# Operand tiles at one place of a 512-byte line, sums rounded together with their residues, and other steps for transposing activations, in a hybrid attention and convolution block

## The chip, the cores and the metric

One core of a Trainium2 chip runs the whole kernel. The metric is the device time of one execution in microseconds; of several runs the median is given. Lower is better.

## The reference

One layer of a streaming encoder on 256 tokens of width 2048, in float32:

```
xn = rms_norm(x) * g1
q, k, v, ga, gg = split(xn @ w_in)            # w_in: 2048 x 5120
att = diff_attention(rope(norm(q)), rope(norm(k)), v)       # 4 heads
u   = silu(layer_norm(conv31(ga * sigmoid(gg))))            # 1024 channels
h = x + concat(att, u) @ w_out                # w_out: 2048 x 2048
hn = rms_norm(h) * g2
y = h + (silu(hn @ w_gate) * (hn @ w_up)) @ w_down          # hidden width 5632
```

## The kernel before

**Three products for one.** Each weight and each activation is split into a rounded part (`hi`, in the type that TensorE takes in one pass) and a residue (`lo`). A product is hi x hi + lo x hi + hi x lo, so one weight tile is used by three matmuls for each half of 128 tokens. The activation is the stationary operand, 128 x 128; the weight is the moving one, 128 x 512. ACT makes the rounded parts of weights (`round_chunk`, L307: `whi`; `round_pair`, L880 and L881: `wh`) and VectorE (DVE) the residues (`split_chunk`, L316: `wlo`; `split_pair`, L885 and L886: `wl`). In a few chunks the residue is made by ACT and an accumulating DMA on POOL's queue instead (L310, L311).

**A list of chunks.** All matmul work is a list, `chunks`, in the order of the stages: QKV and convolution columns (`w_in`), output projection (`w_out`), and the FFN. `run_chunks` walks it. At step t it first issues `split` of chunk t+2, then `load` and `round` of chunk t+3 (in the FFN blocks; elsewhere both lead by 2), then `multiply` of chunk t. Each engine works its own queue in that order of issue; an instruction that waits holds up those behind it.

**Generators and resumes.** What follows a product (norms, activations, transposes) is written as generators. `resume()` lets each go on to its next `yield`; it is called inside and behind each `multiply`. `lag(n)` yields n times. So a number of lags fixes the place of an instruction in the queues.

**The FFN.** The hidden width is 11 blocks (j = 0 to 10) of 512 columns. Block 0 is plain. Blocks 1 to 10 (`fast_block`) compute gate and up together, with sums and differences of operands as in a Strassen product, in 12 units, in the order `sggsggsuusuu` (block 1: `gugusgsusgsu`). A unit `s` is a pair (`multiply_pair`): seven products of three matmuls (L902, L903, L904), the stationary operands from `fhi` and `flo`, the moving ones from `wh` and `wl`, each of seven slices: three are weights as loaded, four are sums of weights (`wt`, made by DVE at L877 to L879 in `round_pair`). The second product already uses the sums. A unit `g` or `u` has two rows of weights (`multiply_two`, L919, L920, L925: 12 matmuls), the stationary operands from `chi` and `clo`. A pair has four resumes, a two-row unit two: in its middle and at its end.

**PSUM.** There are four banks with the tag `acc` and four with the tag `aux`. A block sums in all eight (`q0` to `q3` are acc, `q4` to `q7` aux). The fourth product of a pair sums in `q3`.

**From block to activation.** `products_done` starts when a block's last pair is done: it copies one bank on ACT (L964), adds the banks on DVE (L966 to L973) and applies silu on ACT (L972, L974). `block_done` starts with the block's last unit and is resumed at once: DVE adds the last two banks (L982), multiplies by the gate (L984), then comes `lag(TO_TRANSPOSE)`, and `transposed` turns 128 x 128 squares by TensorE in two groups of four (L796, into a bank `ps_a`). Each group is rounded by ACT (L798, `ahi`), its residue made by DVE (L800, `alo`). While the next block runs, three aux banks hold its sums, so both groups use the one that is left. Block 0's groups use acc banks.

**Down-projection.** Behind blocks 3, 7 and 10 (`FGROUPS` is 4, 4, 3) the products with `w_down` follow, chunks of two rows of 128 and 12 matmuls (`multiply`, L346, L347, L352), with the transposed activations as stationary operand. They have two resumes each. Those of the last group take the last block's second group in the sixth chunk.

**Where tiles lie.** Tiles of a pool lie one behind the other in each partition's memory, and pools follow each other in the order in which they are opened. By the addresses of the compiled program, the place of a tile's first byte in a line of 512 bytes is 192 for the pools `lhs` (`xhi`, `ahi`, `hhi` and their residues) and `wp` (`raw`, `whi`, `wlo`); behind them comes `small` with 1984 bytes, and so the place is 128 for `early` (`wb`) and for `ffn` (`chi`, `fhi`, `wh`, `wl`, `wt`). In `pre`, the odd sizes of `cw` (992 bytes) and `upad0`, `upad1` (4576 each) leave the stationary operands of `w_out`, `mchi`, `mclo`, `mahi` and `malo`, at 32. The latter two hold the attention output of the first two heads, the former two that of the convolution. All slices used by matmuls are whole steps of 512 bytes.

Of the kernel before, what the change touches and what calls it, by code (L numbers as in the profile page):

```python
# [12 lines left out]
F32 = mybir.dt.float32  # L13
# [5 lines left out]
P = 128  # L19
D = 2048  # L20
S = 256
# [5 lines left out]
CC = 1024  # L27
NCT = CC // P
W = 31
FF = 5632  # L30
KD = D // P
N = 512
EPS = 1e-6
LN_EPS = 1e-5
LAMBDA_INIT = 0.8 - 0.6 * math.exp(0.0)
# [31 lines left out]
FGROUPS = (4, 4, 3)  # L67
# [15 lines left out]

HI_AHEAD, LO_AHEAD = 3, 2

TO_TRANSPOSE = 5


def rope_constants():
# [10 lines left out]
def tile_block(  # L100
# [6 lines left out]
    act, dve, pool, pe, sp = nc.scalar, nc.vector, nc.gpsimd, nc.tensor, nc.sync  # L107

    const = ctx.enter_context(tc.tile_pool(name="const", bufs=1))
    lhs = ctx.enter_context(tc.tile_pool(name="lhs", bufs=KD // 2))  # L110
    wp = ctx.enter_context(tc.tile_pool(name="wp", bufs=4))
    small = ctx.enter_context(tc.tile_pool(name="small", bufs=4))
    early = ctx.enter_context(tc.tile_pool(name="early", bufs=2))
    prestack = ExitStack()
    pre = prestack.enter_context(tc.tile_pool(name="pre", bufs=2))
# [12 lines left out]
    def warm_up(n):  # L128
        warm = aux_ps.tile([P, N], F32, tag="aux", name="ps_warm")
        for _ in range(n):  # L130
            pe.transpose(warm[:, :P], ident, ident)
# [9 lines left out]
    def gain_columns():  # L141
        ps = aux_ps.tile([P, N], F32, tag="aux", name="ps_cols")
        pe.transpose(ps[:, :NR], rows, ident[:NR, :NR])
        act.copy(cols, ps[:, :NR])
# [1 line left out]
    def col(key, k):  # L146
        return cols[:, AT[key] + k : AT[key] + k + 1]

    cw = pre.tile([P, NCT, W], F32, tag="cw", name="cw", bufs=1)
    gcs = {}  # L150
    neg_lam = const.tile([P, 1], F32, tag="neg_lam", name="neg_lam")
    cw_rows = [pre.tile([W, N], F32, tag="va", name="cw_rows") for _ in range(CC // N)]
    rt = pre.tile([P, NM, 2, DH], F32, tag="vb", name="rt")
# [3 lines left out]
    def late_loads():  # L157
        flat = conv_w.rearrange("o w i c -> (o w i) c")
        for i in range(CC // N):
            sp.dma_start(out=cw_rows[i], in_=flat[:, i * N : (i + 1) * N])  # L160
        for t, v in ((gb, vecs[:2]), (lamv, vecs[2:])):
# [3 lines left out]
    def late_constants():  # L165
        late_loads()
        yield from lag(4)
        pw = aux_ps.tile([P, N], F32, tag="aux", name="ps_cw")
        for ct in range(NCT):
# [31 lines left out]
    def rsqrt_mean(dst, ss, n, eps):  # L201

        k = dst.shape[-1]
        t = small.tile([P, 8], F32, tag="rsq", name="rsq")
        pool.tensor_scalar(t[:, :k], ss, 1.0 / n, eps, ALU.mult, ALU.add)
        pool.tensor_tensor(dst, t[:, :k], neghalf[:, :k], ALU.pow)
# [8 lines left out]
    def lhs_two(pfx, k):  # L215
        return tuple(lhs.tile([P, 2, S], F32R, tag=f"l{x}", name=f"{pfx}{x}{k}") for x in ("hi", "lo"))
# [20 lines left out]
    def lag(n):  # L237
        for _ in range(n):
            yield
# [182 lines left out]
    def x_rest():  # L422
# [9 lines left out]
        for m in range(NM):  # L432
            ss = small.tile([P, 1], F32, tag="ss1", name="ss1")
            dve.tensor_reduce(ss, ss1[m], AX.X, ALU.add)
            rsqrt_mean(rstd1[m], ss, D, EPS)
        yield
# [4 lines left out]

    NB = N // P
    HN = N // 2
    upad = [pre.tile([P, NB, S + W - 1], F32, tag=f"upad{b}", name=f"upad{b}", bufs=1) for b in range(CC // N)]
    for b in range(CC // N):
        pool.memset(upad[b][:, :, : W - 1], 0.0)
    y = pre.tile([P, NCT, S], F32, tag="y", name="y", bufs=1)
# [126 lines left out]
    def qk_rows(key, b, m, ps):  # L574
# [6 lines left out]
        f = small.tile([P, G], F32, tag="fq", name="fq")  # L581
        rsqrt_mean(f, ss, DH, EPS)
        pool.tensor_scalar(f, f, rstd1[m], 0.0, ALU.mult, ALU.add)
# [102 lines left out]
    def attend_values(hd):  # L686
# [14 lines left out]
        r = small.tile([P, NM], F32, tag="ro", name="ro")  # L701
        rsqrt_mean(r, ss, E, EPS)
        yield from lag(2)
# [24 lines left out]
    def out_done(n, ps):  # L728
# [26 lines left out]
        if n == D // N - 1:  # L755
            yield
            for m in range(NM):
                ss = small.tile([P, 1], F32, tag="ssh", name="ssh")
                dve.tensor_reduce(ss, ss2[m], AX.X, ALU.add)
                rsqrt_mean(rstd2[m], ss, D, EPS)  # L760
            yield
# [16 lines left out]
    def up_done(j, ps):  # L778
        fp = ffn["pool"]
        yield  # L780
        aa = []
        for m in range(NM):
            a = fp.tile([P, N], F32, tag=f"sum{2 + m}", name="a")
            dve.scalar_tensor_tensor(a, ps[m], rstd2[m], sil[m], ALU.mult, ALU.mult)
            aa.append(a)
        yield
        yield from transposed(j, aa)

    def transposed(j, aa):
        for t in range(N // P // 2):  # L790
            pool_, tag = (aux_ps, "aux") if j else (acc_ps, "acc")
            pt = pool_.tile([P, 2, S], F32, tag=tag, name="ps_a")
            for i in range(2):
                for m in range(NM):
                    c = (2 * t + i) * P
                    pe.transpose(pt[:, i, m * P : (m + 1) * P], aa[m][:, c : c + P], ident)  # L796
            hi, lo = lhs_two("a", j * (N // P) + 2 * t)
            act.copy(hi, pt)  # L798
            yield from lag(2)
            dve.tensor_tensor(lo, pt, hi.bitcast(F32), ALU.subtract)  # L800
            for i in range(2):
                actT[j * (N // P) + 2 * t + i] = (hi[:, i, :], lo[:, i, :])
            yield from lag(2 if j else 1)

# [63 lines left out]
    def round_pair(c):  # L870

        fp = ffn["pool"]
        assert "hi" in forms
        b = c["b"]
        c["t"] = t = fp.tile([P, 4, N], F32, tag="wt", name="wt")
        c["hi"] = fp.tile([P, 7, N], F32R, tag="wh", name="wh", bufs=2)
        dve.tensor_tensor(t[:, 2:4], b[:, 1:3], b[:, 0:1].to_broadcast([P, 2, N]), ALU.subtract)  # L877
        dve.tensor_tensor(t[:, 1], b[:, 1], t[:, 3], ALU.add)
        dve.tensor_tensor(t[:, 0], t[:, 1], b[:, 3], ALU.subtract)  # L879
        act.copy(c["hi"][:, 4:], b[:, 1:])  # L880
        act.copy(c["hi"][:, :4], t)  # L881

    def split_pair(c):
        c["lo"] = ffn["pool"].tile([P, 7, N], F32R, tag="wl", name="wl", bufs=2)
        dve.tensor_tensor(c["lo"][:, 4:], c["b"][:, 1:], c["hi"][:, 4:].bitcast(F32), ALU.subtract)  # L885
        dve.tensor_tensor(c["lo"][:, :4], c["t"], c["hi"][:, :4].bitcast(F32), ALU.subtract)  # L886
# [44 lines left out]
    def fast_block(j, order, after_down):  # L931

        units, sums = [], {}
        left = dict(s=list(range(NS)), g=list(TWOS), u=list(TWOS))
        for kind in order:
            what = left[kind].pop(0)
            c = dict(kind=kind, sums=sums, done=None, first={}, last={})
            if kind == "s":
                c.update(k=what, col=j * N, load=load_pair, round=round_pair, split=split_pair,
                         multiply=multiply_pair, uses=[q for q, _, _ in PRODUCTS], products=PRODUCTS)  # L940
            else:
                c.update(ks=what, w=w_gate if kind == "g" else w_up, nk=2, width=N, cols=[(j * N, N)],
                         rows=slice(what[0], what[1] + 1, what[1] - what[0]), by_dma=j > 1 and what in BY_DMA,
                         load=load_chunk, round=round_chunk, split=split_chunk, multiply=multiply_two,
                         uses=(Q3, QX) if kind == "u" else (Q2, Q4))
            units.append(c)
        assert not any(left.values())
        if after_down:

            units[0]["products"] = PRODUCTS[4:] + PRODUCTS[:4]  # L950
        for q in range(8):
            users = [c for c in units if q in c["uses"]]
            users[0]["first"][q] = users[-1]["last"][q] = True
        [c for c in units if c["kind"] == "s"][-1]["done"] = products_done
        units[-1].update(done=lambda sums: block_done(j, sums), prompt=True)
        chunks.extend(units)
# [20 lines left out]
    def block_done(j, q):  # L977
        while "g" not in halfway:
            yield
        g, u = halfway.pop("g"), halfway.pop("u")  # L980
        for m, i in enumerate((Q3, QX)):
            dve.tensor_tensor(u[m], q[i], u[m], ALU.add)  # L982
        for m in range(NM):
            dve.tensor_tensor(u[m], u[m], g[m], ALU.mult)  # L984
        yield from lag(TO_TRANSPOSE)
        yield from transposed(j, u)

    def down_done(g, n, ps):
# [82 lines left out]
```

## Time and profile before

| | |
|---|---|
| median of 3 runs | 1084.51 us (1084.17 to 1084.56) |
| the profiled execution | 1082.97 us, span 1081.2 us |
| mean granted TensorE clock | 0.994 |
| QKV, convolution, attention | about 7 to 252 us |
| output projection | about 252 to 352 us |
| FFN block 0 | about 352 to 398 us |
| blocks 1 to 3, down-projection | 398 to 534, 534 to 622 us |
| blocks 4 to 7, down-projection | 622 to 793, 793 to 881 us |
| blocks 8 to 10, down-projection | 881 to 1008, 1008 to 1077 us |

The profile's busy share of TensorE counts modelled ends of pipelined matmuls; the distance from one start to the next tells the pace. A row of the timeline has the start in us, the duration in us, the engine, the line with the operation, what is written from what is read, the shape, how many instructions are merged, and in brackets the idle time before with what ended it. A row of the windows has the stretch, its length, busy time of TensorE with its count, granted clock, DMA share and GB/s. A row of the waits has the sum in us, the count and the longest.

### The profile page before, as it was taken

How to read it: one execution, taken by the hardware profiler on the slowest of the kernel's cores; microseconds unless marked ns; L12 is line 12 of the kernel's file. 1: busy time of each engine (PE TensorE's matmuls, PEld its weight loads, DVE VectorE, ACT ScalarE, POOL GpSimd, SP SyncE). 2: the span in 40 equal slices, each digit the busy share in tenths (PEclk: the TensorE clock that was granted, in tenths of full speed). 3: DMA queues.
4: the chain of work that ended last, by engine and by line, in shares of the span. 5: the costliest groups of instructions: out<-in, count | busy, mean ns of one | idle time of the engine just before them, and what ended most of it. 6: DMA issues, size and time to landing. Idle time of an engine off the chain costs nothing.

```text
span 1081.2 us, 13236 instructions
## 1 busy us (share of the span) xinstructions
PE 1058.5 (98%) x4834; PEld 871.7 (81%) x4834; DVE 844.8 (78%) x1025; ACT 587.0 (54%) x765; POOL 62.9 (6%) x101
## 2 busy tenths in 40 slices
PE   7999999999999999999999999999999999999998
PEld 7888888877888887788888888878788888887786
DVE  4799989898765689988754699889865589898553
ACT  6544567755765655555443456554643355556332
POOL 0030021200100000000000000000000000000000
PEclk9999999999999999989999999999999999999999
DMA  8856655454345565576555776767566568675661
GB/s 244 258 178 201 190 186 172 151 167 156 137 156 195 163 240 201 195 215 194 175 200 189 238 252 211 214 202 238 164 195 215 201 216 249 220 221 161 220 220 62
DMA packets 120941, 212.45 MB, mean 196 GB/s; under 512 B 7220, under 2 KB 29166, under 8 KB 120876
## 3 DMA queue, kind: packets, MB, share of 16 engines
q1 hardware_dynamic: 117744, 200.56, 56.0%
q0 software_dynamic: 3072, 11.01, 4.9%
q8 instruction: 38, 0.62, 0.2%
q14 instruction: 27, 0.22, 0.1%
q10 hardware_dynamic: 60, 0.03, 0.0%
HBM read 200.04 MB, written 2.10 MB: 187 GB/s over the span
## 4 chain that ended last, share of the span: by engine, by line
PE 79%; DVE 10%; issue 4%; ACT 3%; DMA 2%; POOL 1%; SPq 0%; DVEq 0%; ACTq 0%
PE acc L347 16%; PE acc L346 16%; PE acc L352 16%; PE q L919 5%; PE q L920 5%; PE q L902 5%; PE q L904 5%; PE q L903 5%; PE q L925 5%; DVE wlo L316 3%; ACT wh L881 2%; DVE wt L877 1%; DVE y L483 1%; DMA h<-in_x_dram 1%; PE ps_a L796 1%
## 5 line engine op out<-in xcount | busy, mean ns | idle before, releaser
L316 DVE TENSOR_TENSOR wlo<-raw,whi 128x1024 fp32r<-128x1024 f32 (+1 forms) x279 | 337.6, 1218 | 138.0 <-ACT whi L307 138.0
L307 ACT CAST whi<-raw 128x1024 fp32r<-128x1024 f32 (+1 forms) x297 | 309.3, 1049 | 234.1 <-PE acc L347 166.4
L347 PE MATMUL acc<-whi,alo 128*128 128x512 f32 x384 | 149.6, 390 | 2.3 <-DVE alo L800 2.3
L346 PE MATMUL acc<-whi,ahi 128*128 128x512 f32 x384 | 149.6, 390 | 0.0
L881 ACT CAST wh<-wt 128x2048 fp32r<-128x2048 f32 x40 | 76.6, 1914 | 127.3 <-DVE wt L879 127.3
L346 PE MATMUL acc<-whi,xhi 128*128 128x512 f32 (+1 forms) x352 | 129.8, 375 | 3.9 <-ACT xhi L221 2.8
L347 PE MATMUL acc<-whi,xlo 128*128 128x512 f32 (+1 forms) x352 | 128.2, 371 | 0.5 <-DVE xlo L222 0.4
L919 PE MATMUL q<-whi,chi 128*128 128x512 f32 x320 | 125.7, 393 | 0.0
L920 PE MATMUL q<-whi,clo 128*128 128x512 f32 x320 | 125.4, 392 | 0.0
L902 PE MATMUL q<-wh,fhi 128*128 128x512 f32 x280 | 112.4, 402 | 2.2 <-DVE alo L800 2.2
L904 PE MATMUL q<-wl,fhi 128*128 128x512 f32 x280 | 111.2, 397 | 1.4 <-DVE wl L886 1.4
L903 PE MATMUL q<-wh,flo 128*128 128x512 f32 x280 | 110.6, 395 | 0.0
L483 DVE SCALAR_TENSOR_TENSOR y<-upad,cw,y 128x256 f32<-128x256 f32 x240 | 103.4, 481 | 2.2 <-ACT y L476 1.7
L352 PE MATMUL acc<-wlo,ahi 128*128 128x512 f32 x384 | 103.6, 391 | 0.0
L886 DVE TENSOR_TENSOR wl<-wt,wh 128x2048 fp32r<-128x2048 f32 x40 | 91.6, 2290 | 9.2 <-ACT wh L881 9.2
L352 PE MATMUL acc<-wlo,xhi 128*128 128x512 f32 (+1 forms) x352 | 88.2, 375 | 1.2 <-DVE wlo L316 1.2
L925 PE MATMUL q<-wlo,chi 128*128 128x512 f32 x320 | 87.1, 394 | 0.0
L347 PEld LDWEIGHTS acc<-whi,alo 128*128 128x128 f32 x384 | 72.1, 188 | 17.6 <-DVE alo L800 2.6
L346 PEld LDWEIGHTS acc<-whi,ahi 128*128 128x128 f32 x384 | 72.1, 188 | 15.2 <-ACT ahi L798 0.2
L352 PEld LDWEIGHTS acc<-wlo,ahi 128*128 128x128 f32 x384 | 71.6, 188 | 14.5
L346 PEld LDWEIGHTS acc<-whi,xhi 128*128 128x128 f32 x352 | 66.3, 188 | 15.8 <-ACT xhi L221 3.2
L347 PEld LDWEIGHTS acc<-whi,xlo 128*128 128x128 f32 x352 | 66.3, 188 | 11.9 <-DVE xlo L222 0.9
(194 smaller groups left out, 1416.6 us busy)
## 6 DMA issues: line engine op xcount, KB each, us to landing
raw<-in_w_down_dram SPq DMA_DIRECT2D x88, 512.0 KB, 3.9
raw<-in_w_in_dram SPq DMA_DIRECT2D x48, 512.0 KB, 3.5
raw<-in_w_gate_dram SPq DMA_DIRECT2D x48, 512.0 KB, 4.4
raw<-in_w_up_dram SPq DMA_DIRECT2D x48, 512.0 KB, 3.5
wb<-in_w_up_dram SPq DMA_DIRECT2D x40, 512.0 KB, 3.8
wb<-in_w_gate_dram SPq DMA_DIRECT2D x40, 512.0 KB, 5.6
raw<-in_w_out_dram SPq DMA_DIRECT2D x32, 512.0 KB, 3.5
raw<-in_w_in_dram SPq DMA_DIRECT2D x62, 256.0 KB, 3.4
```

The source lines that it names most:

```text
L307: act.copy(c["hi"], c["raw"])
L316: dve.tensor_tensor(c["lo"], c["raw"], c["hi"].bitcast(F32), ALU.subtract)
L346: pe.matmul(ps[m], xhi[:, ms], hi[:, j, :], start=c["first"] and j == 0, stop=False)
L347: pe.matmul(ps[m], xlo[:, ms], hi[:, j, :], start=False, stop=False)
L352: pe.matmul(ps[m], xhi[:, ms], lo[:, j, :], start=False, stop=c["last"] and j == nk - 1)
L483: dve.scalar_tensor_tensor(y[:, ct, :], src, wk, y[:, ct, :], ALU.mult, ALU.add)
L902: pe.matmul(ps, fhi[:, f, p, :], c["hi"][:, w], start=bool(first), stop=False)
L903: pe.matmul(ps, flo[:, f, p, :], c["hi"][:, w], start=False, stop=False)
L904: pe.matmul(ps, fhi[:, f, p, :], c["lo"][:, w], start=False, stop=bool(last))
L919: pe.matmul(ps, x1[:, ms], hi[:, i, :], start=i == 0 and bool(c["first"].get(q)), stop=False)
L920: pe.matmul(ps, x2[:, ms], hi[:, i, :], start=False, stop=False)
L925: pe.matmul(sum_bank(c, q), forms["plain"][k][0][:, ms], lo[:, i, :], start=False, stop=i == 1 and bool(c["last"].get(q)))
```

## The change

- `small` is opened ahead of `lhs`, and `cw` and `upad` are padded to whole lines of 512 bytes. By the sizes above, all operand tiles then begin at place 128.
- ACT's rounding of the four sums of a pair (L881) is issued in `split_pair`, one step later, right ahead of the residues that use it, instead of in `round_pair`.
- The lags around the transposes change. Behind `block_done`: 4 resumes instead of 5; between a group's rounding and its residue 2 as before; from there to the second group 4 instead of 2. For the blocks ahead of a down-projection and for block 0 (`FIRSTS` is 1, 4, 8, 11, compared with j + 1): 3, 1 and 1 (block 0 has no first lag; it had 2 and 1).

```diff
+LINE = 128
-TO_TRANSPOSE = 5
+FIRSTS = [1] + [sum(FGROUPS[: g + 1]) for g in range(len(FGROUPS))]
...
+    small = ctx.enter_context(tc.tile_pool(name="small", bufs=4))
     lhs = ctx.enter_context(tc.tile_pool(name="lhs", bufs=KD // 2))
     wp = ctx.enter_context(tc.tile_pool(name="wp", bufs=4))
-    small = ctx.enter_context(tc.tile_pool(name="small", bufs=4))
...
-    cw = pre.tile([P, NCT, W], F32, tag="cw", name="cw", bufs=1)
+    cw = pre.tile([P, LINE * 2], F32, tag="cw", name="cw", bufs=1)[:, : NCT * W].rearrange("p (c w) -> p c w", c=NCT)
...
-    upad = [pre.tile([P, NB, S + W - 1], F32, tag=f"upad{b}", name=f"upad{b}", bufs=1) for b in range(CC // N)]
+    UP = NB * (S + W - 1)
+    upad = [pre.tile([P, -(-UP // LINE) * LINE], F32, tag=f"upad{b}", name=f"upad{b}", bufs=1)[:, :UP].rearrange(
+        "p (c s) -> p c s", c=NB) for b in range(CC // N)]
...
     def transposed(j, aa):
+        last = j + 1 in FIRSTS
...
             act.copy(hi, pt)
-            yield from lag(2)
+            yield from lag(1 if last else 2)
             dve.tensor_tensor(lo, pt, hi.bitcast(F32), ALU.subtract)
...
-            yield from lag(2 if j else 1)
+            yield from lag(1 if last else 4)
...
         act.copy(c["hi"][:, 4:], b[:, 1:])
-        act.copy(c["hi"][:, :4], t)
 
     def split_pair(c):
+        act.copy(c["hi"][:, :4], c["t"])
         c["lo"] = ffn["pool"].tile([P, 7, N], F32R, tag="wl", name="wl", bufs=2)
...
-        yield from lag(TO_TRANSPOSE)
+        yield from lag(3 if j + 1 in FIRSTS else 4)
         yield from transposed(j, u)
```

## The prediction

> **What bounds the kernel now.** I read the page first (shares, slices, chain), then the timeline, then the waits.
>
> ```profile
> span 1081.2 us, 13236 instructions
> PE 1058.5 (98%) x4834; PEld 871.7 (81%) x4834; DVE 844.8 (78%) x1025; ACT 587.0 (54%) x765; POOL 62.9 (6%) x101
> ...
> DVE  4799989898765689988754699889865589898553
> ...
> PE 79%; DVE 10%; issue 4%; ACT 3%; DMA 2%; POOL 1%; SPq 0%; DVEq 0%; ACTq 0%
> ```
>
> TensorE is busy 98% of the span and holds 79% of the chain, so two things pay: a faster pace of its matmuls, and fewer waits. VectorE (DVE) has the next 10%, in the stretches where its digits stand at 8 and 9: the FFN blocks 1 to 10.
>
> The pace is read from starts in the timeline, since the ends of matmuls are modelled.
>
> ```profile
> 562.47 0.39 PE L346 MATMUL acc<-whi,ahi 128*128 128x512 f32 x1
> ...
> 576.07 0.39 PE L346 MATMUL acc<-whi,ahi 128*128 128x512 f32 x1
> ...
> 311.30 0.39 PE L346 MATMUL acc<-whi,mchi 128*128 128x512 f32 x1
> ...
> 316.93 0.39 PE L346 MATMUL acc<-whi,mchi 128*128 128x512 f32 x1
> ...
> 508.10 0.40 PE L919 MATMUL q<-whi,chi 128*128 128x512 f32 x1
> ...
> 510.87 0.39 PE L919 MATMUL q<-whi,chi 128*128 128x512 f32 x1
> ...
> 513.61 0.40 PE L902 MATMUL q<-wh,fhi 128*128 128x512 f32 x1
> ...
> 516.38 0.39 PE L902 MATMUL q<-wh,fhi 128*128 128x512 f32 x1
> ...
> 518.42 0.40 PE L919 MATMUL q<-whi,chi 128*128 128x512 f32 x1
> ```
>
> Down-projection, both operands at place 192: five chunks of 12, 60 matmuls in 13.60 us, 226.7 ns each. w_out on `mchi`, places 192 and 32: 24 in 5.63 us, 234.6 ns. A two-row unit, places 192 and 128: 2.77 us for 12 behind a pair, 2.74 us behind another such unit (230.8 and 228.3 ns). A pair, all at 128: its first 12 matmuls take 2.77 us, its last 9 take 2.04 us, 226.7 ns. So equal places run at 226.7 ns, whether 128 or 192, after a run-in; unequal ones do not.
>
> The waits, in block 6 (the two later rows are the same place in blocks 7 and 10):
>
> ```profile
> 717.47 1.22 DVE L316 TENSOR_TENSOR wlo<-raw,whi 128x1024 fp32r<-128x1024 f32 x1
> ...
> 717.69 0.42 PE L904 MATMUL q<-wl,fhi 128*128 128x512 f32 x1
> ...
> 718.61 0.68 DVE L800 TENSOR_TENSOR alo<-ps_a,ahi 128x512 fp32r<-128x512 f32 x1
> ...
> 719.35 0.66 PE L796 MATMUL ps_a<-ident,sum 128*128 128x128 f32 x4 [1.24 <-DVE alo L800]
> ...
> 724.33 0.69 DVE L800 TENSOR_TENSOR alo<-ps_a,ahi 128x512 fp32r<-128x512 f32 x1 [2.46 <-ACT ahi L798]
> ...
> 763.13 0.66 PE L796 MATMUL ps_a<-ident,sum 128*128 128x128 f32 x4 [1.23 <-DVE alo L800]
> ...
> 978.23 0.66 PE L796 MATMUL ps_a<-ident,sum 128*128 128x128 f32 x4 [1.23 <-DVE alo L800]
> ```
>
> The second four transposes need the one free aux bank, which the first four's residue (`alo`) must leave. 717.69 to 719.35 is 1.66 us where 0.23 was due: 1.43 us lost.
>
> ```profile
> 712.41 0.60 PE L796 MATMUL ps_a<-ident,sum 128*128 128x128 f32 x4
> ...
> 713.78 0.39 PE L919 MATMUL q<-whi,chi 128*128 128x512 f32 x1
> ...
> 707.08 1.27 DVE L982 TENSOR_TENSOR sum<-q,sum 128x512 f32<-128x512 f32 x2
> ...
> 750.86 1.27 DVE L982 TENSOR_TENSOR sum<-q,sum 128x512 f32<-128x512 f32 x2
> ...
> DVE wl L886 <- ACT wh L881: 9.2, 30, 0.3
> ...
> ACT wh L881 <- DVE wt L879: 127.3, 39, 6.0
> ```
>
> From one block's L982 to the next's VectorE takes 43.78 us. TensorE's block at 226.7 ns is 4 pairs of 4.76, 8 units of 2.72 and twice four transposes (712.41 to 713.78 less four matmuls, 0.46): 41.7. So in blocks 5 to 7 VectorE sets the period too; 2.46 us of it is the wait at the second `alo`.
>
> **The change, part by part.**
>
> *Place.* All matmul operands go to 128. w_out on `mchi` and `mahi`: 288 matmuls (12 of its 16 row blocks, 4 column blocks, 2 token halves, 3 products) by 7.9 ns is 2.3, less some 40 that stand next to an interruption, 2.0 us. A block has 4 pairs of 4.81 (513.61 to 518.42) against 4.76, and 8 units of 2.75 against 2.72: 0.45 us; the eight blocks 3 to 10, 3.6 us. The QKV stage and its like have short run-ins after transposes: 0.2. Together 5.8. Bounds: 0 if place is not the cause; nothing below, since 516.38 to 518.42 already runs at 128 at the good pace. I take the full 5.8, the nearest rows being the same instructions at equal places. The Trainium skill (TensorE: Matmul & The Clock Gate, "Step-by-step: what each phase is for") says that loading the next tile's weights steals no read bandwidth from the running matmul, as TensorE has two read ports. By that rule place is worth nothing; 234.6 against 226.7 ns speaks against it.
>
> *Transposes inside the blocks (4, 2, 4 resumes for 5, 2, 2).* The first four come at the end of unit 0 instead of the middle of unit 1; the first `alo` is then queued on VectorE right behind unit 3's residues, ahead of L316; the second four come two products later in unit 3. In block 6 terms `alo` ends 1.14 us earlier and TensorE arrives 1.36 us later: 2.5 us against the 1.24 us wait. Three waits go: 3 x 1.43 = 4.3 us.
>
> *Rounding queued with the residues.* ACT no longer stands in front of `ahi` waiting for the sums, so the 2.46 us wait of the second `alo` goes. L881 still starts only when the sums end, so L886 keeps its 0.31. VectorE's block is then 43.78 - 2.46 + up to 0.31 = 41.3 to 41.6, just under TensorE's 41.7. That cover is 0.1 to 0.4 us thick: past it every further wait of VectorE counts.
>
> ```profile
> 414.17 0.80 PE L902 MATMUL q<-wh,fhi 128*128 128x512 f32 x1 [2.21 <-DVE alo L800]
> ...
> 445.21 0.68 DVE L970 TENSOR_TENSOR sum<-q,sum 128x512 f32<-128x512 f32 x1
> ...
> 446.01 0.43 PE L902 MATMUL q<-wh,fhi 128*128 128x512 f32 x1
> ...
> 448.20 1.28 DVE L984 TENSOR_TENSOR sum<-sum,sum 128x512 f32<-128x512 f32 x2
> ...
> 448.80 0.40 PE L919 MATMUL q<-whi,chi 128*128 128x512 f32 x1
> ...
> 455.19 2.29 DVE L886 TENSOR_TENSOR wl<-wt,wh 128x2048 fp32r<-128x2048 f32 x1 [0.32 <-ACT wh L881]
> ...
> 457.54 0.49 PE L904 MATMUL q<-wl,fhi 128*128 128x512 f32 x1 [1.44 <-DVE wl L886]
> ...
> 459.27 1.11 PE L796 MATMUL ps_a<-ident,sum 128*128 128x128 f32 x4 [1.24 <-DVE alo L800]
> ...
> 465.21 0.39 PE L902 MATMUL q<-wh,fhi 128*128 128x512 f32 x1
> ...
> 413.89:417.30 3.41, 3.13 (x7) 0.50 0.10 19
> ...
> 458.26:465.09 6.83, 5.82 (x16) 0.50 0.78 202
> ```
>
> *Blocks 1 and 2.* At 414.17 block 1 waits 2.21 us for the second `alo` of block 0 (an acc bank), and the clock is then granted at half for 3.41 us: 3.9 us in all. With lags of 1 that `alo` is queued one step earlier and the wait goes. But VectorE works on without a gap over 0.32 us until 457.5, so this is not kept: block 2's fourth product must wait for L970 to leave its bank (445.9) whenever TensorE comes, and unit 3's second product for L886 at 457.5. What changes is after 457.54: no wait for `alo`, and no half clock. From 457.54 to 465.21 TensorE does 13 matmuls and four transposes, 3.4 us at full pace, in 7.67: 4.3 us won. Against it: TensorE now idles up to 3.9 us before 446.0. A half-clock window would cost 1.7 us, but TensorE has 0.7 us to spare at the transposes (moved to 448.8, L984 ends at 449.5) and about 1.0 at 457.5. I deduct 0.3 for a second one.
>
> The skill's rule (same page, "HAM oscillation") would have no such window below about 3.4 us of idle time; by the row at 413.89 a wait of 2.21 us was enough, and the row decides.
>
> ```profile
> 538.48 1.28 DVE L984 TENSOR_TENSOR sum<-sum,sum 128x512 f32<-128x512 f32 x2
> ...
> 538.80 1.07 PE L352 MATMUL acc<-wlo,ahi 128*128 128x512 f32 x4
> ...
> 1025.58 0.50 PE L347 MATMUL acc<-whi,alo 128*128 128x512 f32 x1 [2.31 <-DVE alo L800]
> ```
>
> *Last blocks (3, 1, 1).* For block 10 the second `alo` now comes three chunks ahead of its use: the wait of 2.31 us (2.5 with the restart) goes. But the first transposes move from the middle of the third chunk behind the block to the middle of the second (538.80 behind block 3), where L984 ends only at 539.76: 0.96 us of new wait, in blocks 3, 7 and 10: 2.9. The net is a loss of 0.3, bounds +2.5 (if L984 comes earlier) and -0.4.
>
> *Nothing else.* The same DMAs are issued in the same order on SP and POOL; they follow the buffers, which come free no later. Padding adds no instruction.
>
> **Sum.** 5.8 + 4.3 + 4.3 - 0.3 - 0.3 = 13.8 us. The profiled execution takes 1082.97 us (span 1081.2 and 1.8 around it), 1.5 below the median of the runs, 1084.51; that offset I carry over: 1084.5 - 13.8, about 1071.
>
> **The rivals.**
> Place does nothing: no 5.8, the time is 1076.8. For it: the run-in inside a pair at equal places shows that something besides place matters. Against: the 24 matmuls on `mchi` never settle. By the skill's rule above it would be this. Chance 0.17.
> VectorE stays the bound in blocks 5 to 7, 9 and 10, its 2.46 us coming back at another queue (for instance behind ACT's `ahi`): lost are the 4.3 and 5 x 0.45, the time is 1077.5. For it: only 0.1 to 0.4 us of cover. Chance 0.13, a third of it together with the first (1083).
> Slower: the rounding now starts late. L881 is queued behind whatever the step before put on ACT, and L886 waits for it. The point is 13.8 us over 40 pairs, 0.34 us more for each than now. If ACT were each time inside a chunk's cast (1.05 us), VectorE's block would be 41.6 + 4.2 = 45.8, and blocks 3 to 10 each 4.1 us over the 41.7 of the forecast: 33 us, about 1104. Against it: ACT idles before L881 in 39 of 40 pairs now, 3.3 us each. Chance 0.08.
> Better: the new wait at the transposes does not show, or VectorE's chain in block 1 shortens: about 1066. Chance 0.10.
> The forecast itself: 0.52, its own range 1067 to 1075.
>
> **Numbers.** Predicted 1071; the range 1064 to 1079 leaves out the slower case, the joint one and the tails. 0.2%, 2.2 us, is about what a measurement of this kernel tells from no change. Faster by more: 0.52 + 0.17 + 0.10 and two thirds of the 0.13, about 0.88; the same 0.04; slower 0.08.
>
> **What would show it.** w_out chunks on `mchi` 2.72 us apart instead of 2.81, two-row units 2.72. No wait of L796 on `alo` in blocks 6, 7 and 10; L800 without its 2.46 us; L982 to L982 about 41.7. In block 2 still a wait near L886, but full clock behind it. A wait of about 1 us of L796 on L984 in the second chunk behind blocks 3, 7 and 10, and none at L347 in the last. Wrong it would be if L886 shows waits over 0.34 us in most pairs, or if the new idle time in block 2 costs several half-clock windows.

## The result and the profile after

The changed kernel takes 1070.70 us (median of 4 runs, 1069.61 to 1071.78); the kernel before, beside it on the same chip, 1084.34 us (4 runs, 1083.65 to 1084.56). The ratio is 0.988 (95% interval 0.986 to 0.989): 13.6 us less. The profiled execution took 1070.69 us with a span of 1068.8.

Line numbers have moved: L346, L347, L352 are now L349, L350, L355; L902 to L904 are L908 to L910; L919, L920, L925 are L925, L926, L931; L796, L798, L800 are L802, L804, L806; L886 is L892, L881 is L889 (now in `split_pair`), L879 is L885; L964, L966, L970 are L970, L972, L976; L982 and L984 are L988 and L990; L307, L311 and L316 are L310, L314 and L319.

The page after: span, busy shares, VectorE's slices, and the shares of the chain.

```profile
span 1068.8 us, 13235 instructions
PE 1051.6 (98%) x4834; PEld 869.4 (81%) x4834; DVE 845.1 (79%) x1025; ACT 589.3 (55%) x765; POOL 62.7 (6%) x101
...
DVE  4799988899675689999655599999864579998553
...
PE 84%; DVE 8%; ACT 3%; issue 2%; POOL 1%; DMA 1%; SPq 0%; DVEq 0%; ACTq 0%
```

TensorE's share of the chain rose from 79 to 84%, VectorE's fell from 10 to 8% with the same busy time (844.8 and 845.1 us): not VectorE's work became less, but the time that TensorE stood still for it.

The pace, in the timeline after: first and last row of two chunks of `w_out` (24 matmuls), of two two-row units behind a pair (24), of the pair behind them (21), and of 21 chunks of the first down-projection (252).

```profile
311.83 0.39 PE L349 MATMUL acc<-whi,mchi 128*128 128x512 f32 x1
...
317.29 0.39 PE L349 MATMUL acc<-whi,mchi 128*128 128x512 f32 x1
...
503.19 0.39 PE L925 MATMUL q<-whi,chi 128*128 128x512 f32 x1
...
508.63 0.39 PE L908 MATMUL q<-wh,fhi 128*128 128x512 f32 x1
...
513.39 0.39 PE L925 MATMUL q<-whi,chi 128*128 128x512 f32 x1
...
545.06 0.39 PE L349 MATMUL acc<-whi,ahi 128*128 128x512 f32 x1
...
602.18 0.39 PE L349 MATMUL acc<-whi,ahi 128*128 128x512 f32 x1
```

That is 5.46 us for 24 (227.5 ns each, before 234.6), 5.44 for 24 (226.7; before 5.51), 4.76 for 21 (226.7; before 4.81) and 57.12 for 252 (226.7, as before).

Block 6, in the timeline and the waits:

```profile
700.41 1.29 DVE L988 TENSOR_TENSOR sum<-q,sum 128x512 f32<-128x512 f32 x2 [0.25 <-PE q L931]
...
710.81 0.68 DVE L806 TENSOR_TENSOR alo<-ps_a,ahi 128x512 fp32r<-128x512 f32 x1
...
714.06 0.60 PE L802 MATMUL ps_a<-ident,sum 128*128 128x128 f32 x4
...
715.32 0.69 DVE L806 TENSOR_TENSOR alo<-ps_a,ahi 128x512 fp32r<-128x512 f32 x1
...
742.17 1.29 DVE L988 TENSOR_TENSOR sum<-q,sum 128x512 f32<-128x512 f32 x2 [0.25 <-PE q L931]
```

```profile
ACT wh L889 <- DVE wt L885: 78.6, 30, 4.1
...
DVE wl L892 <- ACT wh L889: 9.4, 30, 0.3
```

The first `alo` ends at 711.49, 2.6 us ahead of the second transposes at 714.06, which wait for nothing. The second `alo` has lost its 2.46 us. From L988 to L988 are 41.76 us instead of 43.78, and VectorE now waits for TensorE (`q`, L931) there: TensorE has become the bound of these blocks. L892 waits 0.3 us as L886 did, in 30 pairs.

Block 2, in the timeline; then the windows of a stretch at the start-up and of this stretch (behind the length: busy time and count of TensorE's matmuls and weight loads, VectorE, ACT, POOL, granted clock, DMA share, GB/s):

```profile
441.71 0.50 PE L908 MATMUL q<-wh,fhi 128*128 128x512 f32 x1 [1.41 <-ACT sum L970]
...
443.40 0.50 PE L908 MATMUL q<-wh,fhi 128*128 128x512 f32 x1 [0.73 <-DVE sum L972]
...
445.59 0.49 PE L908 MATMUL q<-wh,fhi 128*128 128x512 f32 x1 [0.43 <-DVE sum L976]
...
457.18 0.50 PE L910 MATMUL q<-wl,fhi 128*128 128x512 f32 x1 [0.85 <-DVE wl L892]
```

```profile
15.12:18.54 3.42, 3.42 (x14) 3.19 (x15) 2.86 (x5) 3.31 (x8) 0.00 (x0) 0.50 1.15 297
441.00:462.00 21.00, 18.02 (x77) 13.42 (x78) 20.34 (x25) 11.10 (x13) 1.08 (x1) 1.00 0.58 167
```

VectorE is busy 20.34 of 21 us. TensorE comes early and waits, four times, and the last wait ends at 457.18 where it ended at 457.54 before. Behind it the clock is now full.

Behind block 3, in the timeline (blocks 7 and 10 look alike at 789.19 and 1002.53):

```profile
533.30 1.28 DVE L990 TENSOR_TENSOR sum<-sum,sum 128x512 f32<-128x512 f32 x2
...
534.03 0.14 PEld L802 LDWEIGHTS ps_a<-ident,sum 128*128 128x128 f32 x1 [0.73 <-DVE sum L990]
...
534.63 0.31 PEld L802 LDWEIGHTS ps_a<-ident,sum 128*128 128x128 f32 x3 [0.47 <-DVE sum L990]
```

The transposes wait for the two halves of L990, as the prediction had it. By the starts of the matmuls around them this costs 1.0 us each time (the prediction had 0.96).

Where the 12.4 us between the two spans come from, by the starts of the same matmuls in both timelines (a minus is time lost):

| stretch | predicted | measured |
|---|---|---|
| start-up to the end of QKV | 0.2 | -1.0 |
| w_out | 2.0 | 1.2 |
| blocks 0 to 2 (block 1's wait, given back; block 2) | 4.0 | 4.6 |
| place in blocks 3 to 10 | 3.6 | 3.5 |
| the three waits in blocks 6, 7 and 10 | 4.3 | 4.5 |
| transposes ahead of the down-projections, last wait | -0.3 | -0.4 |
| sum | 13.8 | 12.4 |

The rest up to 13.6 is that the profiled execution of the kernel before was 1.4 us below its median and that of the changed kernel at its median.

### The profile page after: what moved, and what is told of

It is laid out like the page before. It is cut to its first block, busy times and chain, and to the rows that moved or that the text cites. A ratio compares the mean times of both kernels' runs of the same rounds, so it can differ in the third digit from the quotient of the medians.

```text
span 1068.8 us, 13235 instructions
## 1 busy us (share of the span) xinstructions
PE 1051.6 (98%) x4834; PEld 869.4 (81%) x4834; DVE 845.1 (79%) x1025; ACT 589.3 (55%) x765; POOL 62.7 (6%) x101
## 4 chain that ended last, share of the span: by engine, by line
PE 84%; DVE 8%; ACT 3%; issue 2%; POOL 1%; DMA 1%; SPq 0%; DVEq 0%; ACTq 0%
PE acc L355 16%; PE acc L349 16%; PE acc L350 16%; PE q L925 6%; PE q L926 6%; PE q L931 6%; PE q L910 5%; PE q L908 5%; PE q L909 5%; DVE wlo L319 2%; DVE y L488 1%; DMA raw<-in_w_in_dram 1%; PE ps_a L802 1%; ACT whi L310 1%; ACT wh L889 1%
## 5 line engine op out<-in xcount | busy, mean ns | idle before, releaser
L319 DVE TENSOR_TENSOR wlo<-raw,whi 128x1024 fp32r<-128x1024 f32 (+1 forms) x279 | 337.9, 1218 | 142.1 <-ACT whi L310 141.7
L310 ACT CAST whi<-raw 128x1024 fp32r<-128x1024 f32 (+1 forms) x297 | 309.4, 1049 | 244.6 <-PE acc L350 169.0
L349 PE MATMUL acc<-whi,ahi 128*128 128x512 f32 x384 | 149.7, 390 | 0.0
L350 PE MATMUL acc<-whi,alo 128*128 128x512 f32 x384 | 149.5, 389 | 0.0
L349 PE MATMUL acc<-whi,xhi 128*128 128x512 f32 (+1 forms) x352 | 131.0, 378 | 3.8 <-ACT xhi L224 3.0
L350 PE MATMUL acc<-whi,xlo 128*128 128x512 f32 (+1 forms) x352 | 129.4, 374 | 0.4 <-DVE xlo L225 0.4
L925 PE MATMUL q<-whi,chi 128*128 128x512 f32 x320 | 125.3, 391 | 0.0
L926 PE MATMUL q<-whi,clo 128*128 128x512 f32 x320 | 124.6, 389 | 0.0
L889 ACT CAST wh<-wt 128x2048 fp32r<-128x2048 f32 x40 | 76.6, 1915 | 78.6 <-DVE wt L885 78.6
L908 PE MATMUL q<-wh,fhi 128*128 128x512 f32 x280 | 110.1, 393 | 2.6 <-ACT sum L970 1.4
L910 PE MATMUL q<-wl,fhi 128*128 128x512 f32 x280 | 109.5, 391 | 1.0 <-DVE wl L892 1.0
L355 PE MATMUL acc<-wlo,ahi 128*128 128x512 f32 x384 | 103.5, 391 | 0.0
L892 DVE TENSOR_TENSOR wl<-wt,wh 128x2048 fp32r<-128x2048 f32 x40 | 91.6, 2291 | 9.4 <-ACT wh L889 9.4
L355 PE MATMUL acc<-wlo,xhi 128*128 128x512 f32 (+1 forms) x352 | 88.2, 376 | 1.1 <-DVE wlo L319 1.1
L931 PE MATMUL q<-wlo,chi 128*128 128x512 f32 x320 | 85.8, 390 | 0.0
L349 PEld LDWEIGHTS acc<-whi,ahi 128*128 128x128 f32 x384 | 72.1, 188 | 15.0
L350 PEld LDWEIGHTS acc<-whi,alo 128*128 128x128 f32 x384 | 72.1, 188 | 15.0
L355 PEld LDWEIGHTS acc<-wlo,ahi 128*128 128x128 f32 x384 | 71.6, 188 | 14.5
L349 PEld LDWEIGHTS acc<-whi,xhi 128*128 128x128 f32 x352 | 67.4, 191 | 15.5 <-ACT xhi L224 3.4
L350 PEld LDWEIGHTS acc<-whi,xlo 128*128 128x128 f32 x352 | 67.3, 191 | 11.8 <-DVE xlo L225 0.8
```

The lines of the kernel that those rows point to most:

```text
L310: act.copy(c["hi"], c["raw"])
L319: dve.tensor_tensor(c["lo"], c["raw"], c["hi"].bitcast(F32), ALU.subtract)
L349: pe.matmul(ps[m], xhi[:, ms], hi[:, j, :], start=c["first"] and j == 0, stop=False)
L350: pe.matmul(ps[m], xlo[:, ms], hi[:, j, :], start=False, stop=False)
L355: pe.matmul(ps[m], xhi[:, ms], lo[:, j, :], start=False, stop=c["last"] and j == nk - 1)
L908: pe.matmul(ps, fhi[:, f, p, :], c["hi"][:, w], start=bool(first), stop=False)
```

## The experiments

### The parts by themselves

Four kernels, each the kernel before with one or two of the parts; the kernel before took 1084.13 us beside them.

**Place alone.** Only the order of the pools and the padding of `cw` and `upad`:

```diff
+    small = ctx.enter_context(tc.tile_pool(name="small", bufs=4))
     lhs = ctx.enter_context(tc.tile_pool(name="lhs", bufs=KD // 2))
     wp = ctx.enter_context(tc.tile_pool(name="wp", bufs=4))
-    small = ctx.enter_context(tc.tile_pool(name="small", bufs=4))
```

> Only the places are changed (all operands at 128), rounding and lags as before. Theory: a matmul whose two operands lie at one place starts every 226.7 ns, so the w_out chunks on mchi and the two-row units speed up (2.72 us a chunk); but in blocks 6, 7 and 10 VectorE sets the period, so TensorE only waits longer there for the residue of the first transposes. Gain about 1.3 us in w_out and 0.3 to 0.45 in each of blocks 2 (its second half), 3, 4, 7 (second half), 8 and 10 (second half): 3.5 us, 1081. Rival that place does nothing: 1084.4, paces as before. Rival that the parts simply add up: 5.8 us, 1078.6.

Measured: 1080.4 us (1079.1 to 1081.42), ratio 0.9967 (0.9955 to 0.9978). 3.7 us are gained, near the theory's figure, and not the 5.8 of the whole sum. The timeline of block 6:

```profile
714.68 0.50 PE L907 MATMUL q<-wl,fhi 128*128 128x512 f32 x1 [0.31 <-DVE wl L889]
...
716.41 0.66 PE L799 MATMUL ps_a<-ident,sum 128*128 128x128 f32 x4 [1.23 <-DVE alo L803]
...
721.40 0.69 DVE L803 TENSOR_TENSOR alo<-ps_a,ahi 128x512 fp32r<-128x512 f32 x1 [2.46 <-ACT ahi L801]
```

`alo` (L803 here, behind `ahi`, L801) still waits 2.46 us, VectorE's period is still that of before, and what TensorE gains in blocks 6, 7 and 10 comes back as a wait for `wl` (L889 here) that was not there, besides the 1.23 us for `alo`. So the place's full gain per block can be had only with a shorter VectorE.

That the 3.7 us come so near the theory is in part luck. By the starts, `w_out` gains 1.2 us and blocks 3 to 10 together only 1.2. Another 1.4 come in block 2, where in this execution the half clock lasts 3.41 us (457.62 to 461.03) instead of 6.83.

**Rounding alone.** `act.copy(c["hi"][:, :4], ...)` from `round_pair` to `split_pair`, old lags, old places:

```diff
-        act.copy(c["hi"][:, :4], t)
 
     def split_pair(c):
+        act.copy(c["hi"][:, :4], c["t"])
```

> Only the rounding of the sums is queued with the residues; lags and places as before. Theory: ACT no longer holds up the second group's rounding, so VectorE's wait of 2.46 us at the second residue goes, its period falls under TensorE's, and blocks 6, 7 and 10 lose most of their 1.24 us wait: 3 to 4.3 us; block 2 and the last block stay as they were: about 1080.5. Rival that it only moves work: 1084.4. Rival that VectorE waits longer for the late rounding: over 1090.

Measured: 1077.34 us (1075.79 to 1081.78), ratio 0.9941 (0.9923 to 0.9959). The timeline of its block 6:

```profile
717.17 0.68 DVE L800 TENSOR_TENSOR alo<-ps_a,ahi 128x512 fp32r<-128x512 f32 x1
...
718.07 0.60 PE L796 MATMUL ps_a<-ident,sum 128*128 128x128 f32 x4
```

With the old lags the first `alo` ends at 717.85, 0.2 us ahead of the transposes, and their wait is gone: for the three waits the rounding was enough. The start of the next unit gained 1.5 us in each of blocks 6, 7 and 10. The last group's wait at L347 (2.3 us) is still there, and so are those of blocks 1 and 2.

The median is 3 us below the expected 1080.5, and not all of that is the rounding. The runs spread over 6 us, and the profiled one, at 1078.69, is among the slower: its starts gain 4.5 us in the three blocks and 1.3 in block 2, where the half clock lasts 3.41 us (460.71 to 464.12) instead of 6.83; 1.3 are lost up to the end of QKV.

**Lags alone.** The old place of the rounding and of the tiles:

```diff
-            yield from lag(2)
+            yield from lag(1 if last else 2)
...
-            yield from lag(2 if j else 1)
+            yield from lag(1 if last else 4)
...
-        yield from lag(TO_TRANSPOSE)
+        yield from lag(3 if j + 1 in FIRSTS else 4)
```

> Only the lags are changed; rounding of the sums and places as before. Theory: no wait of the second transposes for the first residue, no half clock in block 2 (4.2 us), the last block net -0.4; but ACT still stands before the second group's rounding, VectorE keeps its 2.46 us wait and a period of 43.7, and TensorE waits for the pair's residues (L886's counterpart) instead in blocks 6, 7 and 10, 0.2 to 1.5 us each: 6 us in all, 1078. Rival that the lags alone remove all waits: 8.1 us, 1076.2, as with both.

Measured: 1082.95 us (1082.22 to 1084.3), ratio 0.9993 (0.9984 to 1.0001): 1.2 us, which can't be told from nothing. The expectation was wrong by 5 us. Its timeline, behind the first transposes of block 0 (402.87):

```profile
405.56 1.91 ACT L882 CAST wh<-wt 128x2048 fp32r<-128x2048 f32 x1 [1.91 <-DVE wt L880]
...
407.37 0.58 ACT L799 CAST ahi<-ps_a 128x512 fp32r<-128x512 f32 x1
...
407.98 0.69 DVE L801 TENSOR_TENSOR alo<-ps_a,ahi 128x512 fp32r<-128x512 f32 x1 [2.46 <-ACT ahi L799]
...
410.26 2.28 DVE L887 TENSOR_TENSOR wl<-wt,wh 128x2048 fp32r<-128x2048 f32 x1
...
412.60 0.50 PE L905 MATMUL q<-wl,fhi 128*128 128x512 f32 x1 [0.86 <-DVE wl L887]
```

Read it from the top: ACT waits 1.91 us at the rounding of the sums (L882 here), `ahi` stands behind it in ACT's queue, VectorE waits 2.46 us for `ahi`, the pair's residues (L887) stand behind that, and TensorE waits for them. The earlier `alo` has put VectorE's wait ahead of work that TensorE needs; TensorE thus waits for `wl` in 11 places, 5.5 us in all. The waits of this kernel and of the next one (both lags and rounding) show it over the whole span:

```profile
DVE alo L801 <- ACT ahi L799: 21.0, 11, 2.5
```

```profile
DVE alo L801 <- ACT ahi L799: 2.5, 8, 0.5
```

21.0 us in 11 waits against 17.2 in 7 before, and 2.5 in 8 once the rounding has moved as well.

**Rounding and lags, old places.** Both of the two diffs above.

> Rounding queued with the residues and the new lags, places as before (192, 128, 32). Theory: the waits of the second transposes in blocks 6, 7 and 10 go (4.3 us), the half clock in block 2 goes (4.2), the last block gains 2.5 and three new waits of 0.96 us behind blocks 3, 7 and 10 cost 2.9: 8.1 us, 1076.2; the paces stay at 234.6 ns for mchi and 2.75 us for a two-row unit. Rival that place did all: 1084.4. Rival that the two halves add up to the whole: 13.6 less what the places alone give.

Measured: 1074.53 us (1074.17 to 1075.37), ratio 0.9914 (0.9901 to 0.9927): 9.6 us where 8.1 was expected, and 3.7 by place alone make 13.3 of the whole change's 13.6. Rounding and lags by themselves made 6.8 and 1.2 by the medians, less than the 9.6 together; the intervals (4.4 to 8.3 and -0.1 to 1.7) don't settle whether the two parts need each other.

### Is it VectorE that holds blocks 1 and 2, and L990 that holds the transposes?

Three kernels built on the changed one, beside the kernel before at 1084.32 us (the last one at 1084.16).

**First transposes one chunk later** behind blocks 3, 7 and 10:

```diff
-        yield from lag(3 if j + 1 in FIRSTS else 4)
+        yield from lag(5 if j + 1 in FIRSTS else 4)
```

> The changed kernel, with five resumes instead of three between the last products of blocks 3, 7 and 10 and the first four transposes, which so come one chunk of the down-projection later. The theory (in the changed kernel these transposes wait for L990, the gate's multiplication on VectorE, 0.47 + 0.49 us at 533.34, 788.5 and 1001.85) expects the three waits of L802 gone and nothing in their place, since the second residue still comes two chunks ahead of its use: 3 x 0.96 = 2.9 us less, about 1067.8. Rival: the second residue of the last group is now late again, as in the kernel before (2.5 us at L347 there, L350 here): the gain is 0.4 at most, 1070.3 or more.

Measured: 1067.44 us (1067.21 to 1067.96), ratio 0.9846 (0.9832 to 0.9861), 3.3 us below the changed kernel. Its timeline behind block 3:

```profile
532.95 1.28 DVE L990 TENSOR_TENSOR sum<-sum,sum 128x512 f32<-128x512 f32 x2
...
535.94 0.60 PE L802 MATMUL ps_a<-ident,sum 128*128 128x128 f32 x4
```

L990 ends at 534.23, 1.7 us ahead of the transposes. From the end of block 3 to the end of the kernel the starts gain 3.0 us, 1.0 for each of the three places, and no wait of L350 for `alo` is in its waits. The theory holds; the three waits were avoidable, and the change had put them there.

**Two residues of block 1 off VectorE.** The last `g` and the last `u` unit take their residue by ACT and an accumulating DMA, as in blocks 2 to 10:

```diff
-                         rows=slice(what[0], what[1] + 1, what[1] - what[0]), by_dma=j > 1 and what in BY_DMA,
+                         rows=slice(what[0], what[1] + 1, what[1] - what[0]), by_dma=j > 0 and what in BY_DMA,
```

> The changed kernel, with the residues of block 1's last g and u units made by ACT and an accumulating DMA, as in blocks 2 to 10: VectorE does two L319 of 1.22 us less in the stretch from 398 to 457. The theory (VectorE's chain, without gaps up to 457, gives back what block 1 gained) expects block 2's fourth unit to start 2.4 us earlier and the waits of L908 and L910 there to shrink by as much: about 1068.3. Rival: the stretch is bound by something else, ACT or the order of the transposes: the waits stay and the time is within 0.5 us of 1070.7.

Measured: 1068.79 us (1067.97 to 1069.69), ratio 0.9861 (0.9845 to 0.9877), 1.9 us below the changed kernel by the medians; the two intervals overlap, so the starts have to tell. By them, 1.45 us are gained between 398 and block 2's fifth unit, of the 2.4 that VectorE saves; the rest of the difference between the two traces, 1.15 us, lies ahead of block 1, where this execution has no half clock at the start-up. No matmul of block 2 waits any more; there is one new wait, in block 1:

```profile
432.75 1.19 PE L931 MATMUL q<-wlo,chi 128*128 128x512 f32 x4 [2.51 <-DMA wlo<-raw]
```

```profile
433.83:437.24 3.41, 3.41 (x10) 2.67 (x9) 3.12 (x3) 3.05 (x3) 0.05 (x1) 0.50 1.02 293
```

The accumulating DMA, issued at 424.38, comes later than the residue by VectorE would have, and (second fence, a window) the clock is granted at half for 3.41 us behind this wait. So TensorE comes to block 2 later than in the changed kernel (by 2.3 us, counted from the start of block 1), runs through it at its own pace and leaves it 1.45 us earlier: VectorE's chain was the bound there. That no wait is left in block 2 comes in part from TensorE's late arrival: the late DMA with its half clock takes the rest of the gain.

**Both.** 

> The changed kernel with both additions: the first transposes behind blocks 3, 7 and 10 one chunk later, and the residues of block 1's last g and u units by ACT and an accumulating DMA. The stretches don't meet, so the gains should add up: 3.2 and 1.9 us as measured by themselves, about 1065.6. Rival: the transfers on POOL's queue or the start of block 2 shift the phase of blocks 3 to 10 so that another wait appears: 1067 or more.

Measured: 1066.33 us (1065.47 to 1066.88), ratio 0.9834 (0.982 to 0.9848), the fastest version. It lies 4.4 us below the changed kernel, where 5.2 was the sum of the two; the intervals of this and of the first overlap, so how much the second adds to the first (1.1 us by the medians, 1.7 by the starts between 414 and 461) isn't settled.

### What place counts?

Four kernels: the changed one with two unused tiles between the pools, so that `lhs` (stationary operands of QKV, block 0 and the down-projections), `wp` (`whi`, `wlo`) and `ffn`, `early`, `pre` lie apart. The pace in the timeline is what counts here, more than the time. The edit, with 64 and 16 floats for the first:

```diff
     lhs = ctx.enter_context(tc.tile_pool(name="lhs", bufs=KD // 2))
+    ctx.enter_context(tc.tile_pool(name="gap_a", bufs=1)).tile([P, 64], F32, tag="gap_a", name="gap_a")
     wp = ctx.enter_context(tc.tile_pool(name="wp", bufs=4))
+    ctx.enter_context(tc.tile_pool(name="gap_b", bufs=1)).tile([P, 16], F32, tag="gap_b", name="gap_b")
```

**256 and 64 apart.**

> The changed kernel with unused tiles between the pools: lhs stays at place 128, wp (raw, whi, wlo) lies at 384, and ffn, early and pre at 448. So the two operands are 256 bytes apart in the QKV stage, block 0 and the down-projections (some 2300 matmuls), and 64 apart in two-row units and in w_out on the convolution's output. Theory A (the distance in a line of 512 bytes counts): at 64 apart the pace of the kernel before, about 229 ns against 227; at 256 apart some pace above 227, by the rows of 64 and 160 apart 1.6 to 7.9 ns more: 4 + 4 to 4 + 18 us, 1079 to 1093. Rival B (a line of 128 bytes or less counts): 256 apart runs like equal, 226.7 ns, and only the 4 us of 64 apart come: about 1075. Rival C (only what lies in the same pool or was opened in that order counts): no change, 1070.7.

Measured: 1076.88 us. In its timeline, first and last row of the 21 down-projection chunks (256 apart) and of 24 two-row matmuls (64 apart); L351, L927 and L910 of these four kernels are L349, L925 and L908 of the changed one:

```profile
545.02 0.39 PE L351 MATMUL acc<-whi,ahi 128*128 128x512 f32 x1
...
602.14 0.39 PE L351 MATMUL acc<-whi,ahi 128*128 128x512 f32 x1
...
624.63 0.39 PE L927 MATMUL q<-whi,chi 128*128 128x512 f32 x1
...
630.23 0.39 PE L910 MATMUL q<-wh,fhi 128*128 128x512 f32 x1
```

57.12 us for 252, exactly as at equal places: a line of 512 bytes, as the title has it, is not what counts. 64 apart costs more here (5.60 us for 24, 233.3 ns) than in the kernel before (5.51): there the stationary operand lay 64 below the moving one, here 64 above.

**128 and 192 apart** (32 and 48 floats).

> As the run with 256 and 64 bytes, with lhs at place 128, wp at 256, ffn, early and pre at 448: 128 apart in QKV, block 0 and the down-projections, 192 apart in two-row units and in w_out on the convolution's output. Theory A (a line of 512 bytes): both slower than equal, 128 apart between the 1.6 ns of 64 and the 7.9 ns of 160, and 192 apart at least as slow as 160: 2300 x 1.6 to 7.9 ns and (768 + 288) x 7.9 ns, 4 + 8 to 18 + 8 us: 1083 to 1097. Rival B (a line of 128 bytes): 128 apart runs like equal and 192 like 64: about 1075.

Measured: 1082.72 us.

```profile
545.46 0.39 PE L351 MATMUL acc<-whi,ahi 128*128 128x512 f32 x1
...
604.01 0.39 PE L351 MATMUL acc<-whi,ahi 128*128 128x512 f32 x1
```

58.55 us for 252, 232.3 ns: 128 apart is not like equal, so a line of 128 bytes is out too. The two-row units at 192 above have a median of 5.51 us for 24, as in the kernel before at 64 below: the same place in a line of 256 bytes.

**32 and 256 apart** (8 and 64 floats).

> As the run with 256 and 64 bytes, with lhs at place 128, wp at 160, ffn, early and pre at 416: the stationary operand lies 32 bytes below the moving one in QKV, block 0 and the down-projections (taken in a line of 256, at 224), and 256 above it in two-row units and in w_out on the convolution's output. Theory D, from the medians of the runs so far (stationary less moving operand, in a line of 256 bytes: 0 runs at 227 ns, 64 at 233, 96 at 234, 128 at 232, 192 at 229): 224 lies between 192 and 256, so 227 to 229 ns, and two-row units at 227: 0 to 2300 x 2 ns = 4.6 us more than the changed kernel, 1071 to 1075.5. Rival A (a line of 512): 256 apart slows the two-row units: 768 x 2 to 7 ns more, 1.5 to 5 us on top.

Measured: 1080.21 us, above the expected 1071 to 1075.5. The two-row units, 256 apart, take 5.44 us as at equal places; theory D's line of 256 bytes holds. But the down-projection, at 32 below:

```profile
545.30 0.39 PE L351 MATMUL acc<-whi,ahi 128*128 128x512 f32 x1
...
604.11 0.39 PE L351 MATMUL acc<-whi,ahi 128*128 128x512 f32 x1
```

58.81 us, 233.4 ns. The expectation had read a value between those of 192 and 256; the smaller step costs more.

**160 and 32 apart** (40 and 8 floats): the distance of `w_out` before, now in the other stages.

> lhs at place 128, wp at 288, ffn, early and pre at 320: the stationary operand lies 160 bytes below the moving one in QKV, block 0 and the down-projections, as in the kernel before only in w_out, and 32 above it in two-row units and in w_out on the convolution's output. Theory D expects 234 ns where w_out had it, now in QKV, block 0 and the down-projections: 2300 x 7 ns = 16 us, and 227 to 233 ns at 32 above: 1056 x 0 to 6 ns = 0 to 6 us; together 1087 to 1093. Rival (the 234 ns of w_out came from something else in that stage, the interruptions or the mixture of four operands): QKV and the down-projections stay near 227 to 229 ns, 1071 to 1077.

Measured: 1088.89 us, within the expected 1087 to 1093.

```profile
545.59 0.39 PE L351 MATMUL acc<-whi,ahi 128*128 128x512 f32 x1
...
604.63 0.39 PE L351 MATMUL acc<-whi,ahi 128*128 128x512 f32 x1
...
631.93 0.40 PE L927 MATMUL q<-whi,chi 128*128 128x512 f32 x1
...
637.53 0.39 PE L910 MATMUL q<-wh,fhi 128*128 128x512 f32 x1
```

59.04 us for 252, 234.3 ns, as `w_out` had before (234.6); and 5.60 us for 24 two-row matmuls at 32 above. So the cost goes with the places of the two operands and not with the stage. Put together, by the stationary operand's place less the moving one's, in a line of 256 bytes:

| 0 | 32 | 64 | 96 | 128 | 192 | 224 |
|---|---|---|---|---|---|---|
| 226.7 ns | 233.3 | 233.3 | 234.3 | 232.3 | 229.6 | 233.4 |

0 is measured at 0 and at 256 apart, 192 at 64 below and 192 above, 96 in `w_out` of the kernel before and in the last run; 32, 64, 128 and 224 in one run each. Other widths of tiles were not tried, and what in the chip makes the place count is not shown.

## Why the prediction was right, point by point

- **The bound.** The reading (TensorE's pace and waits; VectorE beside it in the FFN blocks) held at each place where a part was taken alone.
- **Place.** The mechanism was right: all operands at one place run at 226.7 ns. Blocks 3 to 10 gave 3.5 us for the forecast 3.6. The term for `w_out` was mis-sized: 1.2 instead of 2.0. The prediction took 7.9 ns for all but 40 of the 288 matmuls; the 12 by 12 rows of the steady stretch agree (234.6 to 227.5, 7.1 ns), but the products are interrupted by transposes and attention products, on `mahi` in most chunks: the 96 matmuls there gained 0.27 us, 2.8 ns each, those on `mchi` 1.03 us, 5.4 ns each, interruptions included (one of them was 0.14 us longer). A run-in of about a dozen matmuls behind each interruption is about as slow at equal places as before. The rule of the Trainium skill that the prediction weighed (TensorE: Matmul & The Clock Gate, "Step-by-step: what each phase is for": loading weights takes no read bandwidth from the running matmul) would have left the pace as it was. These runs do not agree: with nothing but addresses changed, the same 252 matmuls take 57.12 to 59.04 us.
- **The rival "VectorE stays the bound"** was right for place alone (blocks 6, 7 and 10 gained nothing) and for the lags alone, wrong for the whole: the move of the rounding removes the 2.46 us that it needed. The prediction gave the three waits to the lags. Either part is enough for them: with the lags alone, too, no wait of the transposes for `alo` is left in the waits, but new ones for `wl` take their place; the rounding alone removes them and adds none. (The price of 1083 for this rival together with the first does not come out of its terms: 1071, 5.8 and 4.3 make 1081.)
- **The slower rival.** L889 on ACT is not late: VectorE waits 0.3 us for it in 30 pairs as before, and ACT itself still waits up to 4.1 us for the sums.
- **Blocks 1 and 2.** As forecast, the 2.2 us wait and the half clock of block 1 go, and VectorE's chain gives them back: TensorE is 4.2 us ahead of the kernel before up to 432 us, 0.3 behind it at 455, and 4.5 us ahead again behind block 2's fourth unit. No second half-clock window came in this execution, so the deducted 0.3 was not needed; where one came, in the run with the later transposes, it cost nothing (last section). With two residues off VectorE, TensorE came to block 2 later and still left it 1.45 us earlier, which shows the chain as the bound.
- **Last blocks.** Each of the three new waits is 1.0 us, the last wait of L350 is gone: -0.4 for -0.3 (the prediction's own terms, 2.5 less 2.9, make -0.4). The run with the later transposes shows them to be these waits' cost.
- **Not foreseen:** 1.0 us at the start-up. The execution has a half-clock window at 15.12 to 18.54 us that the profiled execution before hadn't. It comes and goes: the runs of place alone, of the lags alone and of the later transposes have none there, the one of the rounding alone has it (1.3 us). So the sum of 13.8 is 1.4 more than the 12.4 us between the spans. The prediction also carried over to the changed kernel that the profiled execution lay 1.5 us below the median, and there it lay at the median. The two errors cancel: that 1071 and 1070.70 are so near is luck, where 12.4 for 13.8 is the fair measure of the sum.

## What to carry to other kernels

When matmuls of one shape have several paces in one timeline, compare the addresses of their two operands; here padding to a common place in a line of 256 bytes was worth 3 to 8 ns of 227 per matmul. A faster TensorE pays only where no other engine's period is as long: see from one block's instruction to the next's on the other engine, and shorten that too. When a step is moved earlier in a queue, look at what its input waits for on the engine before: a wait that was harmless at the end of the queue holds up everything queued behind its new place.

## What was not expected of the hardware

The table of places above: 32 bytes apart costs as much as 64 or 96, and the sign counts (64 above 233.3 ns, 64 below 229.6).

The half clock is not a fixed price of a wait. In its 17 runs beside the first experiments the kernel before took from 1081.63 us at a mean clock of 0.999 to 1086.02 at 0.991. The run with the later transposes has the changed kernel's code up to block 3 and the same wait ahead, in its timeline and the windows:

```profile
441.35 0.50 PE L908 MATMUL q<-wh,fhi 128*128 128x512 f32 x1 [1.40 <-ACT sum L970]
```

```profile
443.69:447.11 3.42, 3.42 (x10) 2.33 (x9) 3.32 (x7) 1.30 (x3) 0.00 (x0) 0.50 0.44 144
```

There 3.42 us at half clock follow; in the changed kernel's own execution, behind 1.41 us at 441.71, the clock is 1.00. It cost nothing in the end: the two executions are 0.36 us apart at the start of this unit and again behind the wait for `wl` at 457, since VectorE was the bound. The Trainium skill (TensorE: Matmul & The Clock Gate, "HAM oscillation — how this bites in real kernels") has a rule of no idle gaps above some 3.4 us. The length of these windows agrees with that figure; the waits that went ahead of them (1.4 us here, 2.2 in block 1 before) are shorter.

The traces say more on what decides it, though no run was made to test it. Within an execution the changes of the clock lie whole steps of 3.41 us apart (in the kernel before, 417.30 to 458.26 is twelve), and in another execution the steps lie elsewhere. The step ahead of the half clock in the run with the later transposes, and then the least busy of these steps past the start-up in the changed kernel (TensorE's busy time and count, clock, DMA share, GB/s):

```profile
440.28:443.69 3.41, 1.62 (x6) 1.00 0.86 300
```

```profile
438.37:441.78 3.41, 2.00 (x10) 1.00 0.46 117
```

In the first both waits fall mostly into one step, in the second they are shared between two. In all thirteen traces, past the first 20 us and up to the end of the work, the half clock followed each full-clock step in which TensorE was busy for 0.8 to 1.74 us (11 of them) and none with 1.81 us or more. At the start-up this does not hold: a step with 1.46 us at 11.11 in the kernel before was not followed by it. So the busy share of a fixed step fits these traces, and not the length of a single wait; it is a reading, not a test.
